# Gate, query and key projections of a decoder block in seven block products instead of eight, as a stage of their own

## The chip, the cores and the metric

One core of a Trainium2 chip runs the whole program. The metric is the device time of one execution in microseconds; shown are the median and the extremes of several executions, and one further execution that was profiled.

## The reference, cut to what matters

1024 tokens of width 1024 go through one layer: a gated linear attention (GLA) of 4 heads, three groups of dilated attention of 4 heads each, a mix of the two branches by sigmoid gates, and a mixture of 32 experts, 2 to a token. All is float32.

```python
h = rms_norm(x, norm1_g)
gq, gk, gv, gr, ga_lr = parts[:5]          # parts = split(h @ w_in): GLA q, k, v, output gate, decays
log_a = log_sigmoid(ga_lr @ w_gla_a2 + b_gla_a) / 16
o_gla = gla_chunked(heads(gq), heads(gk), heads(gv), heads(log_a))
y_gla = (rms_norm(o_gla) * silu(gr)) @ w_proj_gla
for window, dilation in ((128, 1), (512, 4), (2048, 16)):    # groups 0, 1, 2
    q, k, v = ...                          # q and k are normed per head
    o_g, m_g, d_g = dilated_group(q, k, v, ...)
y_att = combine(outs, maxes, dens) @ w_proj_attn
g_gla, g_att = split(sigmoid(h @ w_branch_gate + b_branch_gate))
x = x + (g_gla * y_gla + g_att * y_att) @ w_out
x = x + hier_moe(rms_norm(x, norm2_g), ...)
```

## The kernel before

Each float32 product is made of three matmuls on rounded parts: every operand is split into a high part and the rest, and `mm3` adds high by high, high by low and low by high into one PSUM tile of 128 partitions by 512 columns. A contraction over 1024 is eight k-steps, so 24 matmuls a tile. Weights come by way of `Weights`: SP issues the load of a unit of 128 by 1024 into `w_raw` (3 buffers); ScalarE rounds it (line 131) and VectorE takes the rest (line 132) into a `part` (5 buffers); `take(n)` hands out n units and prepares up to `ahead` more, four as a rule.

A planner lays the instructions of each engine out in one order, by their place in the program and by when it expects their inputs and buffers; it lets loads and stores run ahead of that place where a buffer is free. At run time every engine, and the queue of transfers that SP issues, keeps that order and waits at semaphores. `run`, `weave` and the generators set the place in the program: `weave(main, fill, n)` takes n steps of `fill`, a k-step of three matmuls each, for every step of `main`.

The stages, in order:

1. Eight token tiles are normed, transposed and split into the strips `hT`, while the first matmuls of the GLA values already run. The values (192 matmuls, strips stationary) stay in SBUF in `kb` tiles.
2. Decays of all four heads (`decays`), with head 0's queries and keys as filling. `heads(h)` makes the transposed queries and keys of a head with `columns`: the weights are stationary, the strips move; 96 matmuls a head.
3. `recur(h)`, the recurrence of head h in 16 steps, filled by `heads(h + 1)`, the last by `k_stage(2)`, the keys of dilated group 2.
4. `attention(g)` for g = 2, 1, 0: the values of the group (192 matmuls with nothing beside them), then queries, scores and values tile by tile, with the next group's keys, or at the end the first three tiles of `gr`, as filling. Outputs go to `oa_dram`, maxima and sums to `st_dram`.
5. `gr`: the GLA output gate, eight tiles, multiplied onto the GLA output into `ogs` (four `ka` and four `kb` tiles). From the maxima and sums of all groups come the factors `f_dram`.
6. The projection `yg` (line 694 on): 16 tiles of 12 matmuls, copied by ScalarE (line 702) and stored in `yg_dram`.
7. `together()` (line 707 on) combines the groups: for each of eight tiles three pairs of loads, of attention outputs and of factors that are spread over all partitions (lines 715 and 717), products on VectorE (line 719), two sums (722, 723) and a split into `oas`, in `ka` and `kb` tiles. It uses the nine `t2k` buffers of 512 columns. It stands in the program between `yg` and the gates.
8. Gates and mixing: for each c of 8, `gates(c, hf)` makes two tiles of 24 matmuls for either half of the tokens and a sigmoid; `mix` makes the attention projection (12 matmuls on four of the `oas`), the gated sum, and stores it in `zt_dram`. Gates of both halves stand ahead of the first `mix`.
9. `out_tile(n)` multiplies by `w_out`; beside it `route(n - 1)` norms the tile, computes router logits (line 884, copied at 887, turned at 890), picks experts and writes slots. For the last tile nothing stands beside it. The first loads of expert weights (`E.load`) are spread over these tiles.
10. 32 experts: a gather by GpSimd (line 992), transposes (line 999), three products with 72 matmuls in all, and an adding scatter.

Buffers are laid out as a stack: the tiles of stages 9 and 10 take the space of those of stages 1 to 8, and each waits only for the tiles that it overlaps.

## Time and profile before

| | |
|---|---|
| median of 3 runs | 1812.63 us (1810.82 to 1814.84) |
| profiled execution | 1810.6 us, of which the span of its instructions 1808.5 us |
| mean granted TensorE clock | 0.992 |
| TensorE, VectorE, ScalarE busy | 97%, 59%, 50% of the span |
| moved by transfers | 324.42 MB, mean 179 GB/s |

Times below count from the start of the span. A row of a timeline gives start, duration, engine, line and what is written from what; matmuls are pipelined, so their durations overlap and the distance of their starts is what one costs. An engine's idle time has a cost only where the engine that sets the end waits for it.

### The profile page before, as it was taken

What the parts mean: (1) busy time and instruction counts of PE and PEld (TensorE: products, weight loads), DVE (VectorE), ACT (ScalarE), POOL (GpSimd) and SP (SyncE); (2) the same over time, 40 slices, a digit from 0 to 9 for tenths busy, and PEclk for the clock granted to TensorE, in tenths of its full rate; (3) what the DMA queues carried; (4) which work ended last, traced back from release to release, by engine and by line L of the source; (5) the groups of instructions that cost most, each with busy time, mean ns of one, the idle gap of its engine ahead of it and who ended that gap; (6) DMA issues with size and microseconds to landing.
All of it is one profiled execution on the core that took longest, in us unless ns stands there. A gap on an engine that the chain in (4) does not pass through costs nothing.

```text
span 1808.5 us, 22835 instructions
## 1 busy us (share of the span) xinstructions
PE 1752.7 (97%) x8473; PEld 1477.2 (82%) x8473; DVE 1060.9 (59%) x1561; ACT 905.9 (50%) x1464; POOL 119.2 (7%) x110
## 2 busy tenths in 40 slices
PE   8999999999999999999999999979999999999995
PEld 6788899999998888887888877757777777777774
DVE  6475550342145225556222266679899989989884
ACT  6453441343244224532211142358888888787783
POOL 0000000000000000000000001121111111121110
PEclk9999999999999999999999999989999999999998
DMA  5111110121102111479222298489999999999991
GB/s 213 47 36 59 47 43 30 51 77 61 47 24 84 48 47 36 131 216 283 72 93 93 66 301 260 150 258 365 360 354 344 356 352 354 349 361 353 358 358 38
DMA packets 123216, 324.42 MB, mean 179 GB/s; under 512 B 25808, under 2 KB 42784, under 8 KB 123088
## 3 DMA queue, kind: packets, MB, share of 16 engines
q1 hardware_dynamic: 112512, 304.83, 47.8%
q0 software_dynamic: 10016, 17.78, 4.1%
q8 instruction: 67, 1.10, 0.2%
q14 instruction: 45, 0.37, 0.1%
q10 hardware_dynamic: 576, 0.34, 0.1%
HBM read 297.49 MB, written 42.43 MB: 188 GB/s over the span
## 4 chain that ended last, share of the span: by engine, by line
PE 85%; DVE 5%; DMA 4%; ACT 3%; issue 2%; SPq 0%; POOL 0%; POOLq 0%; DVEq 0%; ACTq 0%
PE acc L241 21%; PE acc L242 21%; PE acc L243 21%; PE mm L241 3%; PE mm L243 3%; PE mm L242 3%; PE mm L393 2%; PE mm L421 2%; DVE t2k L1011 2%; PE tp L999 1%; PE tp L339 1%; PE mm L594 1%; PE tp L1015 1%; DMA m_raw<-in_w_up_dram 1%; ACT part L131 1%
## 5 line engine op out<-in xcount | busy, mean ns | idle before, releaser
L132 DVE TENSOR_TENSOR part<-w_raw,part 128x1024 fp32r<-128x1024 f32 x114 | 139.3, 1222 | 258.9 <-ACT part L131 258.5
L241 PE MATMUL acc<-part,strip 128*128 128x512 f32 x640 | 276.6, 432 | 0.0
L242 PE MATMUL acc<-part,strip 128*128 128x512 f32 x640 | 257.4, 402 | 0.2 <-DVE part L132 0.2
L243 PE MATMUL acc<-part,strip 128*128 128x512 f32 x640 | 257.1, 402 | 0.0
L132 DVE TENSOR_TENSOR part<-m_raw,part 128x1024 fp32r<-128x1024 f32 x167 | 202.3, 1220 | 24.7 <-ACT part L131 23.6
L131 ACT CAST part<-m_raw 128x1024 fp32r<-128x1024 f32 x167 | 174.5, 1055 | 43.1 <-PE acc L243 31.0
L241 PE MATMUL acc<-strip,part 128*128 128x512 f32 x448 | 181.3, 405 | 1.2 <-ACT t2k L737 1.2
L242 PEld LDWEIGHTS acc<-part,strip 128*128 128x128 f32 x640 | 172.8, 270 | 10.3 <-DVE part L132 0.7
L243 PEld LDWEIGHTS acc<-part,strip 128*128 128x128 f32 x640 | 170.8, 267 | 11.4
L241 PEld LDWEIGHTS acc<-part,strip 128*128 128x128 f32 x640 | 170.7, 267 | 10.6 <-ACT part L131 0.5
L242 PE MATMUL acc<-strip,part 128*128 128x512 f32 x448 | 176.8, 395 | 0.0
L131 ACT CAST part<-w_raw 128x1024 fp32r<-128x1024 f32 x114 | 119.9, 1051 | 113.6 <-PE acc L243 94.5
L243 PE MATMUL acc<-strip,part 128*128 128x512 f32 x448 | 175.2, 391 | 0.0
L243 PE MATMUL acc<-part,xT 128*128 128x512 f32 x320 | 127.2, 398 | 0.0
L242 PE MATMUL acc<-part,xT 128*128 128x512 f32 x320 | 127.0, 397 | 0.0
L132 DVE TENSOR_TENSOR m_part<-m_raw,m_part 128x1024 fp32r<-128x1024 f32 x102 | 124.1, 1218 | 4.7 <-ACT m_part L131 4.4
L241 PE MATMUL acc<-part,xT 128*128 128x512 f32 x320 | 126.6, 395 | 0.0
L131 ACT CAST m_part<-m_raw 128x1024 fp32r<-128x1024 f32 x102 | 107.5, 1056 | 12.7 <-PE acc L243 8.3
L331 DVE TENSOR_REDUCE ss<-t2k 128x4 f32<-128x512 f32 x48 | 32.9, 685 | 133.4 <-ACT t2k L329 133.4
L241 PEld LDWEIGHTS acc<-strip,part 128*128 128x128 f32 x448 | 84.3, 188 | 20.6 <-ACT t2k L737 1.6
L243 PEld LDWEIGHTS acc<-strip,part 128*128 128x128 f32 x448 | 84.2, 188 | 18.3
L242 PEld LDWEIGHTS acc<-strip,part 128*128 128x128 f32 x448 | 84.4, 188 | 17.2 <-issue 1.2
(274 smaller groups left out, 3304.5 us busy)
## 6 DMA issues: line engine op xcount, KB each, us to landing
m_raw<-in_w_gate_dram SPq DMA_DIRECT2D x95, 512.0 KB
m_raw<-in_w_down_dram SPq DMA_DIRECT2D x89, 512.0 KB
m_raw<-in_w_up_dram SPq DMA_DIRECT2D x85, 512.0 KB
w_raw<-in_w_in_dram SPq DMA_DIRECT2D x52, 512.0 KB
w_raw<-in_w_mix_dram SPq DMA_DIRECT2D x32, 512.0 KB
n_raw<-in_w_up_dram SPq DMA_DIRECT2D x26, 512.0 KB
n_raw<-in_w_down_dram SPq DMA_DIRECT2D x22, 512.0 KB
w_raw<-in_w_gate_dram SPq DMA_DIRECT2D x17, 512.0 KB
```

The costliest lines, as they stand in the source:

```text
L131: self.copies.append(self.nc.scalar.copy(hi, raw))
L132: self.last = self.nc.vector.tensor_tensor(lo, raw, hi.bitcast(F32), op=OP.subtract)
L241: nc.tensor.matmul(ps, ah, bh, start=first, stop=False)
L242: nc.tensor.matmul(ps, ah, bl, start=False, stop=False)
L243: nc.tensor.matmul(ps, al, bh, start=False, stop=last)
L331: nc.vector.tensor_reduce(ss, sq.rearrange("p (h e) -> p h e", h=4), axis=AX.X, op=OP.add)
L339: nc.tensor.transpose(pt[:, 128 * h:128 * h + 128], sq[:, 128 * h:128 * h + 128], ident)
L393: nc.tensor.matmul(ps[:, h2, 128 * c:128 * c + 128], qT[:, 128 * h:128 * h + 128], kT[j][:, 128 * h:128 * h + 128], start=True, stop=True)
L421: nc.tensor.matmul(po[:, 128 * h:128 * h + 128], v[j][:, 128 * h:128 * h + 128], pTs[c][:, 128 * h:128 * h + 128], start=c == 0, stop=c == ...
L594: nc.tensor.matmul(pa[:n, t], ek[:, j], qt[:, t], start=True, stop=True)
L999: nc.tensor.transpose(pt[:, 128 * j:128 * j + 128], xg[:, 128 * k:128 * k + 128], ident)
L1011: prod = nc.vector.tensor_tensor(ap.rearrange("t (k p) -> t p k", k=4), a.rearrange("t (p k) -> t p k", k=4), pu.rearrange("t (p k) -> t p ...
```

## The change

The branch gates and the GLA queries and keys leave their stages and get one of their own, after the GLA values. It takes the weights in 12 pairs: two blocks of 128 output columns each (the two gates of one c, or two heads' queries or keys). With the pair as rows, the two halves of the contraction and the two halves of the tokens, each pair is a product of 2 by 2 blocks, done by Winograd's form of Strassen's method with seven block products in place of eight. `seven()` makes the seven left factors from the raw weights on VectorE and splits them; `sums(k)` makes, once for all pairs, four sums of strip parts and their splits, `T`; `winograd()` runs the products and puts the results together on VectorE from PSUM. Queries and keys go to `qk_dram`, sigmoids to `sig_dram`.

Around it: the GLA values go to `v_dram` and come back head by head; decays are made a head ahead within the recurrence; the recurrence is filled with the keys and the values of group 2, by the pattern 2, 2, 2, 1 and through DRAM for the values, which `attention(2)` then loads. The projection multiplies its tiles by the first gate, loaded into `s0`, on VectorE. Mixing runs over the halves of the tokens and then over c, with two loads and a store of 512 columns a round. The strips keep their space at the foot of the stack until the end of mixing. The router's product swaps its operands, which makes the copy and the transpose unnecessary. `warm(n)` issues n matmuls on a constant tile, at the start, beside the last tile's routing and before the experts.

```diff
             lst.append(units(sl(1024, 512), 4))
-            for h in range(4):
-                lst.append(units(np.concatenate([sl(128 * h, 128), sl(512 + 128 * h, 128)]), 2))
+            for h in (0, 2):
+                lst += [units(sl(512 * c + 128 * (h + j), 128), 1) for c in range(2) for j in range(2)]
+            for c in range(8):
+                lst += [wb[c:c + 1], wb[8 + c:9 + c]]
...
+    def raws(self, n):
+        if len(self.loaded) < n:
+            self.load(n - len(self.loaded))
+        got, self.loaded = [r for r, _ in self.loaded[:n]], self.loaded[n:]
+        return got
...
+def feed(main, fill, pattern):
+    i = 0
+    while True:
+        try:
+            next(main)
+        except StopIteration as e:
+            return e.value
+        for _ in range(pattern[i % len(pattern)]):
+            next(fill, None)
+        i += 1
...
     def room(i):
-        return raw.tile([128, 1024], F32, name="w_raw"), part if i < 81 else \
+        return raw.tile([128, 1024], F32, name="w_raw"), part if i not in (77, 78, 79) else \
             (lambda: p4.tile([128, 2, 1024], F32R, name="wo", bufs=3))
-    W = Weights(nc, [w_in[i] for i in range(52)] + [w_mix[i] for i in range(32)], room)
+    W = Weights(nc, [w_in[i] for i in range(68)] + [w_mix[i] for i in range(16)], room, 0)
...
+    still = consts.tile([128, 128], F32, name="still")
+    nc.vector.memset(still, 1.0)
+    def warm(n):
+        ps = acc()
+        for _ in range(n):
+            tc.keep_in_program_order(nc.tensor.matmul(ps[:, 0:128], still, still, start=True, stop=True))
...
+    warm(14)
...
+    units = W.take(4)
+    for b in range(NT):
+        ps = acc()
+        run(project(ps, 0, b, units))
+        t = t2k()
+        nc.scalar.copy(t, ps)
+        nc.sync.dma_start(v_dram[0, b // 2, :, 512 * (b % 2):512 * (b % 2) + 512], t)
...
+    tq = ts.enter_context(tc.tile_pool(name="tq", bufs=16))
+    Y = {(i, j): [tuple(p[:, 512 * j:512 * j + 512] for p in hT[4 * i + k]) for k in range(4)] for i in range(2) for j in range(2)}
...
+    def seven():
+        u, v = W.raws(2)
+        u1, u2, v1, v2 = u[:, :512], u[:, 512:], v[:, :512], v[:, 512:]
+        sums = [t2k() for _ in range(4)]
+        s1, s2, s3, s4 = sums
+        p = [part() for _ in range(4)]
+        W.copies.append(nc.scalar.copy(p[0][:, 0], u))
+        nc.vector.tensor_tensor(p[0][:, 1], u, p[0][:, 0].bitcast(F32), op=OP.subtract)
+        nc.vector.tensor_tensor(s1, v1, v2, op=OP.add)
+        nc.vector.tensor_tensor(s2, s1, u1, op=OP.subtract)
+        nc.vector.tensor_tensor(s3, u1, v1, op=OP.subtract)
+        nc.vector.tensor_tensor(s4, u2, s2, op=OP.subtract)
+        got = [(p[0][:, 0, :512], p[0][:, 1, :512]), (p[0][:, 0, 512:], p[0][:, 1, 512:])]
+        for n, (t, j) in enumerate(((s2, 1), (s3, 1), (s1, 2), (v2, 2), (s4, 3))):
+            c = slice(512 * (n % 2), 512 * (n % 2) + 512)
+            hi, lo = p[j][:, 0, c], p[j][:, 1, c]
+            split(hi, lo, t)
+            got.append((hi, lo))
+        W.load(2 - len(W.loaded))
+        return got
+    def winograd(blocks, scale, use):
+        a11, a12, s2, s3, s1, a22, s4 = blocks
+        def product(w, y):
+            ps = acc()
+            for k in range(4):
+                c = slice(128 * k, 128 * k + 128)
+                mm3(ps, (w[0][:, c], w[1][:, c]), y[k], k == 0, k == 3)
+            return ps
+        def plus(ps, t):
+            r = t2k()
+            nc.vector.scalar_tensor_tensor(r, ps, scale, t, op0=OP.mult, op1=OP.add)
+            return r
+        p1 = t2k()
+        nc.scalar.activation(p1, product(a11, Y[0, 0]), AF.Copy, scale=scale)
+        use(plus(product(a12, Y[1, 0]), p1), 0, 0)
+        x = plus(product(s2, T[2]), p1)
+        t = plus(product(s3, T[3]), x)
+        ps = product(s1, T[1])
+        use(plus(ps, t), 1, 1)
+        y = plus(ps, x)
+        use(plus(product(a22, T[4]), t), 1, 0)
+        use(plus(product(s4, Y[1, 1]), y), 0, 1)
+    T = {i: [] for i in (1, 2, 3, 4)}
+    def sums(k):
+        (h11, l11), (h12, l12), (h21, l21), (h22, l22) = (tuple(p.bitcast(F32) for p in Y[q][k]) for q in ((0, 0), (0, 1), (1, 0), (1, 1)))
+        def parts_of(i, v):
+            t = tq.tile([128, 2, 512], F32R, name="tq")
+            split(t[:, 0], t[:, 1], v)
+            T[i].append((t[:, 0], t[:, 1]))
+        def op(r, a, b, o):
+            nc.vector.tensor_tensor(r, a, b, op=o)
+        v, w = t2k(), t2k()
+        op(v, h22, h12, OP.subtract)
+        op(w, l22, l12, OP.subtract)
+        op(v, v, w, OP.add)
+        parts_of(3, v)
+        v2 = t2k()
+        op(v2, v, h11, OP.add)
+        op(v2, v2, l11, OP.add)
+        parts_of(2, v2)
+        v4 = t2k()
+        op(v4, h21, v2, OP.subtract)
+        op(v4, v4, l21, OP.add)
+        parts_of(4, v4)
+        v1, w1 = t2k(), t2k()
+        op(v1, h12, h11, OP.subtract)
+        op(w1, l12, l11, OP.subtract)
+        op(v1, v1, w1, OP.add)
+        parts_of(1, v1)
+    nxt = seven()
+    for k in range(4):
+        sums(k)
+    def keep_qk(c, h):
+        def use(t, j, hf):
+            nc.sync.dma_start(qk_dram[c, h + j, :, 512 * hf:512 * hf + 512], t)
+        return use
+    def keep_gate(c):
+        def use(t, j, hf):
+            nc.scalar.activation(t, t, AF.Sigmoid, bias=bgate[:, 8 * j + c:8 * j + c + 1])
+            nc.sync.dma_start(sig_dram[j, c, :, 512 * hf:512 * hf + 512], t)
+        return use
+    pairs = [(128.0 ** -0.5 if c == 0 else 1.0, keep_qk(c, h)) for h in (0, 2) for c in range(2)] + [(1.0, keep_gate(c)) for c in range(KT)]
+    for n, (scale, use) in enumerate(pairs):
+        blocks = nxt
+        if n < len(pairs) - 1:
+            nxt = seven()
+        else:
+            W.ahead = 4
+            W.fetch(4)
+        winograd(blocks, scale, use)
+    ts.close()
+    ph.close()
+    ph = ExitStack()
+    work = wide = ph.enter_context(tc.tile_pool(name="work", bufs=2, reuse_waits="tile"))
...
+    def v_stage(g, keep):
+        units = W.take(4)
+        for i in range(NT):
+            ps = acc()
+            yield from project(ps, g, i, units)
+            keep(i, ps)
...
+        if v is None:
+            v = []
+            def keep(i, ps):
+                if i == 0:
+                    run(last)
+                v.append(v[i - 1][:, 512:] if i % 2 else kb4())
+                nc.scalar.copy(v[i][:, :512], ps)
+            run(v_stage(g, keep))
...
         for c in range(2):
-            t = w4k()
-            for hf in range(2):
-                ps = acc()
-                yield from columns(ps, [(units[k // 4][0][:, 256 * (k % 4) + 128 * c:256 * (k % 4) + 128 * c + 128],
-                                         units[k // 4][1][:, 256 * (k % 4) + 128 * c:256 * (k % 4) + 128 * c + 128])
-                                        for k in range(KT)], hf)
-                nc.scalar.activation(t[:, 512 * hf:512 * hf + 512], ps, AF.Copy, scale=128.0 ** -0.5 if c == 0 else 1.0)
-            qk.append(t)
+            qk.append(w4k())
+            nc.sync.dma_start(qk[c], qk_dram[c, h])
...
+    def decays(h):
+        l, vh = kb4(), kb4()
+        for j in range(4):
+            nc.sync.dma_start(vh[:, 256 * j:256 * j + 256].rearrange("p (b e) -> p b e", b=2),
+                              v_dram[0, j].rearrange("p (b e) -> p b e", b=2)[:, :, 128 * h:128 * h + 128])
...
+    def keys_values(g, got):
+        got.append((yield from k_stage(g)))
...
+            t = t2k()
+            nc.scalar.copy(t, ps)
+            nc.sync.dma_start(v_dram[1, i // 2, :, 512 * (i % 2):512 * (i % 2) + 512], t)
...
+        yield from v_stage(g, keep)
...
+    got = []
+    fill = keys_values(2, got)
+    head = [feed(decays(0), fill, (8,))] + heads(0)
...
+        for i, _ in enumerate(main):
+            if i % 3 == 2 and other is not None:
+                try:
+                    next(other)
+                except StopIteration as e:
+                    out, other = out.append(e.value), None
+            yield
...
     for h in range(H):
-        _, qk = weave(recur(h, *qk), heads(h + 1) if h < H - 1 else k_stage(2), 2 if h < H - 1 else 4)
+        nxt = []
+        if h < H - 1:
+            following = heads(h + 1)
+        feed(both(recur(h, *head[0], *head[1:]), decays(h + 1) if h < H - 1 else None, nxt), fill, (2, 2, 2, 1))
+        if h < H - 1:
+            head = nxt + following
+    run(fill)
...
+    for j in range(NT // 2):
+        t = kb4()
+        nc.sync.dma_start(t, v_dram[1, j])
+        v2 += [t[:, :512], t[:, 512:]]
...
-        attention(g, *qk, after)
+        attention(g, *qk, v2 if g == 2 else None, after)
...
-        yt = w4k()
+        yt, s0 = w4k(), w4k()
+        nc.sync.dma_start(s0, sig_dram[0, c])
         for hf in range(2):
...
-            nc.scalar.copy(yt[:, 512 * hf:512 * hf + 512], ps)
+            cols = slice(512 * hf, 512 * hf + 512)
+            nc.vector.tensor_tensor(yt[:, cols], s0[:, cols], ps, op=OP.mult)
         nc.sync.dma_start(yg_dram[c], yt)
...
+    W.ahead = 1
+    wa = W.take(4)
+    for hf in range(2):
+        cols = slice(512 * hf, 512 * hf + 512)
+        for c in range(KT):
+            yt, sg, zt = t2k(), t2k(), t2k()
+            nc.sync.dma_start(yt, yg_dram[c, :, cols])
+            nc.sync.dma_start(sg, sig_dram[1, c, :, cols])
             ps = acc()
-            run(columns(ps, cut(u, 0, KT), hf))
...
-        nc.vector.tensor_tensor(sig[hf, 1], sig[hf, 1], ps, op=OP.mult)
-        nc.vector.tensor_tensor(zt[:, cols], sig[hf, 0], sig[hf, 1], op=OP.add)
-        nc.sync.dma_start(zt_dram[4 * hf:4 * hf + 4, :, c].rearrange("n p t -> p n t"), zt[:, cols].rearrange("p (n t) -> p n t", n=4))
...
+            for h, u in enumerate(cut(wa[c // 2], 4 * (c % 2), H)):
+                mm3(ps, u, oas[2 * h + hf], h == 0, h == H - 1)
+            nc.vector.tensor_tensor(sg, sg, ps, op=OP.mult)
+            nc.vector.tensor_tensor(zt, sg, yt, op=OP.add)
+            nc.sync.dma_start(zt_dram[4 * hf:4 * hf + 4, :, c].rearrange("n p t -> p n t"), zt.rearrange("p (n t) -> p n t", n=4))
...
     ph.close()
+    ph0.close()
...
-            nc.tensor.matmul(pl[:36, 0:128], wr_s[:, k], xts[k // 4][:, 128 * (k % 4):128 * (k % 4) + 128],
+            nc.tensor.matmul(pl[:, 0:36], xts[k // 4][:, 128 * (k % 4):128 * (k % 4) + 128], wr_s[:, k],
                              start=k == 0, stop=k == KT - 1)
-        lt = p4.tile([36, 128], F32, name="lt")
-        nc.vector.tensor_copy(lt, pl[:36, 0:128])
-        yield
-        pt = tp()
-        nc.tensor.transpose(pt[:, 0:36], lt, ident[:36, :36])
...
-        nc.vector.scalar_tensor_tensor(lg[:, 0:4], pt[:, 0:4], rs, br_s[:, 0:4], op0=OP.mult, op1=OP.add)
-        nc.vector.scalar_tensor_tensor(lg[:, 8:40], pt[:, 4:36], rs, br_s[:, 4:36], op0=OP.mult, op1=OP.add)
+        nc.vector.scalar_tensor_tensor(lg[:, 0:4], pl[:, 0:4], rs, br_s[:, 0:4], op0=OP.mult, op1=OP.add)
+        nc.vector.scalar_tensor_tensor(lg[:, 8:40], pl[:, 4:36], rs, br_s[:, 4:36], op0=OP.mult, op1=OP.add)
...
+    def waits():
+        yield
+        warm(15)
+        for _ in range(4):
+            yield
+        warm(4)
+        yield
...
-        _, xt = weave(route(n, xt), out_tile(n + 1) if n < NT - 1 else iter(()), 1)
+        _, xt = weave(route(n, xt), out_tile(n + 1) if n < NT - 1 else waits(), 1)
...
+    warm(36)
```

## Rows read from the trace of the kernel before

**Rows 1.** The page's shares: engine, busy us, share of the span, instructions.
```profile
PE 1752.7 (97%) x8473; PEld 1477.2 (82%) x8473; DVE 1060.9 (59%) x1561; ACT 905.9 (50%) x1464; POOL 119.2 (7%) x110
```
**Rows 2.** Stretches: length, then each engine's busy us, granted clock, transfer share, GB/s.
```profile
120.00:240.00 120.00, 120.00 (x697) 104.32 (x696) 67.46 (x147) 48.57 (x95) 0.00 (x0) 1.00 0.13 45
...
754.00:786.00 32.00, 32.00 (x141) 26.24 (x140) 20.61 (x35) 14.43 (x21) 0.00 (x0) 1.00 0.26 75
786.00:842.00 56.00, 55.56 (x243) 45.26 (x241) 35.56 (x44) 15.61 (x26) 0.00 (x0) 1.00 0.95 282
...
874.00:882.00 8.00, 8.00 (x37) 6.56 (x36) 3.04 (x4) 2.15 (x3) 0.00 (x0) 1.00 0.49 166
882.00:890.00 8.00, 8.00 (x37) 6.56 (x36) 2.77 (x4) 1.23 (x2) 0.00 (x0) 1.00 0.49 158
...
1176.00:1192.00 16.00, 4.56 (x18) 3.83 (x18) 8.03 (x28) 4.12 (x6) 3.54 (x4) 0.56 0.82 266
1200.00:1600.00 400.00, 396.72 (x1816) 316.02 (x1815) 364.83 (x370) 329.49 (x388) 60.02 (x42) 1.00 0.98 353
```
**Rows 3.** TensorE's timeline in the gate stage, the first and the last of 19 matmuls.
```profile
899.83 0.39 PE L241 MATMUL acc<-strip,part 128*128 128x512 f32 x1
...
903.95 0.39 PE L241 MATMUL acc<-ka,part 128*128 128x512 f32 x1
```
**Rows 4.** TensorE's timeline at the start; in brackets the idle time before.
```profile
7.81 1.97 PE L283 MATMUL tp<-mats,w4k 128*128 128x128 f32 x8 [7.81 <-DVE w4k L278]
...
11.82 0.63 PE L242 MATMUL acc<-part,strip 128*128 128x512 f32 x1
```
**Rows 5.** Places on the chain that ended last: start, us on it, what.
```profile
17.99 0.87 PE tp L283 x8
...
124.86 0.89 PE mm L606 x8
...
142.82 0.89 PE mm L606 x8
...
832.54 6.97 DMA t2k<-f_dram
...
1173.49 0.12 DVE lt L887
...
1173.66 0.26 PE tp L890
...
1182.27 7.11 DMA w4k<-h_dram,sidx
```
**Rows 6.** VectorE's timeline: after the norms, at three gating steps, at the seventh split.
```profile
40.91 0.42 DVE L247 TENSOR_TENSOR strip<-tp,strip 128x256 fp32r<-128x256 f32 x1 [0.44 <-ACT strip L246]
60.32 1.23 DVE L132 TENSOR_TENSOR part<-w_raw,part 128x1024 fp32r<-128x1024 f32 x1 [18.99 <-ACT part L131]
...
755.70 0.68 DVE L247 TENSOR_TENSOR ka<-t2k,ka 128x512 fp32r<-128x512 f32 x1
...
756.90 0.68 DVE L668 TENSOR_TENSOR t2k<-t2k,w4k 128x512 f32<-128x512 f32 x1
...
842.11 0.69 DVE L247 TENSOR_TENSOR ka<-t2k,ka 128x512 fp32r<-128x512 f32 x1
```
**Rows 7.** VectorE's instructions by form: count, busy us and mean ns, idle before them.
```profile
L132 DVE TENSOR_TENSOR part<-w_raw,part 128x1024 fp32r<-128x1024 f32 x114 | 139.3, 1222 | 258.9 <-ACT part L131 258.5 <-issue 0.3
...
L719 DVE TENSOR_TENSOR t2k<-t2k 128x512 f32<-128x512 f32 x24 | 22.8, 955 | 19.8 <-DMA t2k<-f_dram 19.8
...
L544 DVE TENSOR_TENSOR_SCAN ka<-t2k 128x128 f32<-128x128 f32 x32 | 11.0, 404 | 0.2
L745 DVE TENSOR_TENSOR t2k<-t2k,acc 128x512 f32<-128x512 f32 x16 | 11.0, 685 | 16.4 <-PE acc L243 16.4
```
**Rows 8.** TensorE's timeline where the gate matmuls begin.
```profile
824.92 0.39 PE L241 MATMUL acc<-strip,part 128*128 128x512 f32 x1
```

More of the change, by code (lines that the diff above doesn't have):

```diff
@@ L93, in _layout @@
     lst = [pair(wg, c) for c in range(0, 8, 2)]
-    for c in range(8):
-        lst += [wb[c], wb[8 + c]]
-        if c % 2 == 0:
-            lst.append(pair(wa, c))
+    lst += [pair(wa, c) for c in range(0, 8, 2)]
     out["w_mix"] = np.stack(lst + list(a["w_out"].reshape(8, 128, 1024)))
@@ L204, in w4k @@
     def w4k(shape=(128, 1024), dt=F32):
-        return work.tile(list(shape), dt, name="w4k", bufs=n4k)
+        return wide.tile(list(shape), dt, name="w4k", bufs=n4k)
     def ka4(shape=(128, 1024), dt=F32):
@@ L357, in k_stage, with attention @@
         return kT, last
-    def attention(g, kT, last, after):
+    def v_stage(g, keep):
[4 more added lines that the diff above has]
+            keep(i, ps)
+    def attention(g, kT, last, v, after):
         bias = w4k((128, 4, 256))
@@ L363, in attention @@
         sd = work.tile([128, NT, 2, 4], F32, name="sd", bufs=2)
-        units = W.take(4)
-        v = []
-        for i in range(NT):
-            ps = acc()
-            run(project(ps, g, i, units))
-            if i == 0:
-                run(last)
-            if i % 2 == 0:
-                t = kb4()
-            v.append(t[:, 512 * (i % 2):512 * (i % 2) + 512])
-            nc.scalar.copy(v[i], ps)
+        if v is None:
[6 more added lines that the diff above has]
+            run(v_stage(g, keep))
         units = W.take(4)
@@ L478, in attention @@
             nc.sync.dma_start(st_dram[g], sn)
-    units = W.take(4)
-    v = []
-    for b in range(NT):
-        ps = acc()
-        run(project(ps, 0, b, units))
-        if b % 2 == 0:
-            t = kb4()
-        v.append(t[:, 512 * (b % 2):512 * (b % 2) + 512])
-        nc.scalar.copy(v[b], ps)
     wr = t2k((128, 128))
```

102 lines of the change are left out of this document (40 added, 62 removed).

## The prediction

> **What bounds the kernel now.** I read the shares first: TensorE is busy 97% of the span [rows 1]. Then the stretches [rows 2], for idle time and for what fills the other engines. Through the recurrence (120 to 240 us) TensorE never waits, with VectorE at 56%; from 786 to 842 us it loses 0.44 us although the transfer engines are full; through the experts, with transfers full again, under 1%. Only between the last tile and the experts (1176 to 1192 us) is it idle, busy 4.56 of 16 us at a granted 0.56. So a matmul that goes is worth its own time, unless something that it covered comes out. What it covers I looked for on the chain of waits and in VectorE's order of time.
>
> **The removed matmuls.** A pair of weight blocks took 8 products of 4 k-steps of 3 matmuls, 96; now 7, 84. Of 12 pairs (8 of gates, 4 of queries and keys), 144 matmuls of 512 columns go. In the gate stage 18 of them start within 903.95 - 899.83 = 4.12 us [rows 3], 0.229 us each: -33.0 us. The rows hold the stationary and moving kinds of the new phase, so I keep that rate. All other matmuls of 512 columns only move.
>
> **The opening.** Early matmuls last 0.63 us where the gate stage has 0.39 [rows 3, 4], and eight transposes take 1.97 us [rows 4], later 0.87 [rows 5]: the start runs at 1.2 GHz. Fourteen dummy matmuls are put ahead of it. Some seven slow matmuls at 0.2 us: -1.5 us; from 0, if the first tile's transfers hold it anyway, to -2.5.
>
> **Sums of the block phase.** VectorE's last instruction on the normed strips starts at 40.91 us, and it then rests 19 us [rows 6]: that is the cover. Every sum reads the last token tile, so none starts before 41.3 us. Each k takes 10 adds or subtractions and 4 splits, 14 instructions at 0.60 us start to start (755.70 to 756.90 are two steps [rows 6]), 8.4 us; four k take 34 us, and the five half splits of the first weights, whose buffers come free only as the value stage ends, 3 us: until about 78 us. The value stage's matmuls end near 62 us, two products need no sums (24 x 0.229 = 5.5 us), and the third wants its fourth k at 69 us, which VectorE has at about 74. Then the product results, which VectorE must read out of three PSUM buffers, queue behind the sums still left. I take +8 us: from 0 (results first, sums in between) to 14 (sums and the next pair's weights all ahead). Later pairs are covered: 1.22 + 9 x 0.60 + 7 x 0.69 = 11.5 us of VectorE [rows 6, 7] against 84 x 0.229 = 19.2 us of TensorE. The phase's weights and stores, 25 MB in 231 us, are 110 GB/s where 282 have been carried [rows 2]: nothing.
>
> **The recurrence.** Its filling goes from 2 steps of 3 matmuls for each of its own to 1.75, and decays, key norms and weight splits come beside it. A half of a head takes 142.82 - 124.86 = 18.0 us [rows 5], a head 36; at 56% VectorE has 20 us of that, 18 without splits. Decays add two instructions of 0.69 and eight scans of 0.40 us [rows 7], 4.6; norms about 5, splits 2.4: 30 us, 83%. TensorE has no wait there at 56%; I allow +3 us, from 0 to 10. Keys, queries and values are loaded a head ahead, on SP's queue, where only the stores of keys and values stand before them: nothing, or a few us at the first head, inside that bound. The value stage that leaves group 2's attention costs the same in its new place.
>
> **Where the gates ended.** This is the largest unknown. The stage that combines the three attention groups fetches 24 pairs of transfers and made the seventh of its eight tiles at 842.11 + 0.69 us [rows 6]; the projection stage ended at 824.9, where gate matmuls began [rows 8]. The 96 gate matmuls ahead of the first mixing product were the cover. They are gone, and mixing wants four of the combined tiles at once, the seventh among them. Unchanged transfers leave 842.8 - 824.9 - 2 (the first nine matmuls) = 16 us of wait. More come in: half of the sigmoids beside the projection, then two loads and a store of 256 KB for each of 16 rounds of 12 x 0.229 = 2.75 us. From 786 us on I count 22 pairs, 11.5 MB, at 282/0.95 = 297 GB/s, and 21.5 MB of others (4.2 of products stored, 2.6 of sigmoids not yet fetched, 4.2 + 4.2 + 4.2 for mixing, 2.1 of weights) at the 330 GB/s of a full share that 874 to 890 us show [rows 2]: 39 + 65 = 104 us, to 890. Matmuls alone would end at 824.9 + 192 x 0.229 = 868.9. So +21 us; from 2 (transfers drawn ahead into 754 to 786 us, whose share is 0.26 [rows 2]) to 45 (the second rival). VectorE now reads the projection's results too, in order behind instructions that waited 19.8 us for transfers [rows 7]; three PSUM buffers cover 5.5 us of a wait, and the rest is caused by the same transfers, already counted.
>
> Nine buffers serve the rounds. A load took 6.97 us from its issue [rows 5]; with VectorE's steps of 0.69 us a round holds them for about 7.7 + 8.4 + 7.7 us, 2.6 us over nine, just under 2.75. The Trainium skill ("DMA: Bandwidth & Descriptors", Anatomy of one DMA) puts a transfer at some 2 us plus its bytes over 436 GB/s, an estimate of 2.6 us for 256 KB, by which a round needs 1.2 us and the buffers never bind. The loaded queue here shows 6.97, so I keep the row.
>
> **The end of routing.** A copy and a transpose leave the chain of each tile (from 1173.49 until 1173.66 + 0.26 [rows 5]): 0.4 us at the last tile, covered by output matmuls at the others. Dummy matmuls keep TensorE at work there. The 4.56 us in 1176 to 1192 would be 2.6 us at the full level (0.56 of 4.56), eight further transposes some 1.1 us less (1.97 against 0.87 [rows 4, 5]): with the 0.4, and a little for the matmuls after them, -4 us, from -2 (the dummies end too early) to -6. The 36 before the experts last about 8 us, if a product of this width costs 2 x 0.11 us as two transposes do [rows 5]; that is inside the wait for the first gather, 7.11 us from 1182.27 [rows 5], within 1 us. Experts and the loads that wait for their buffers start that much earlier, so it is passed on in full.
>
> **The sum**: -33.0 - 1.5 + 8 + 3 + 21 - 4 = -6.5 us. The profiled execution took 1810.6 us (span 1808.5), 2.0 below the median of 1812.6; from the one 1804, from the other 1806. I predict **1805 us**.
>
> **Rivals.**
> *Mixing opens without a wait* (2 in place of 21). The combining stage was in no hurry, with 96 gate matmuls behind it; buffers or the queue's order, not bandwidth, held it before 786 us. For it: the share of 0.26 just before. Against it: 0.95 right after. 19 us less: 1786.
> *Transfers bound projection and mixing outright*; this is the one on the other side. Its place is 786 to 890 us. The strips lie free there now, so expert and output tiles that are laid over them can be fetched at once: up to 13 transfers of 0.5 MB, 6.8 MB, 21 us at 330 GB/s, ahead of what mixing waits for. Then 21 becomes 42 to 45 and the time 1829. The slower sign starts from 32 us of wait on. For it: a full share already stands there; against it: loads for later stages may be ordered behind.
> *Sums and recurrence at their upper ends* (14 and 10 for 8 and 3): 13 us more, 1818.
> *The block form saves nothing*: if half of the weights of each pair are late by 2.8 us, 12 pairs eat the 33 us and the time is 1838. The 7.7 us of VectorE that each pair leaves over speak against it; I count it with the third.
>
> **Chances.** Forecast 0.44 (1796 to 1812 by its own terms), open mixing 0.24 (1778 to 1796), transfers 0.24 (1814 to 1834), late sums 0.08. 0.2% of 1812.6 is 3.6 us, about what can be told from no change. Faster: 0.24 and three quarters of 0.44, 0.57. Same: a fifth of 0.44, a tenth of 0.24, half of 0.08, 0.15. Slower: the rest, 0.28. The range leaves a tenth out on each side: 1782 to 1830.
>
> **What would show it.** 144 fewer matmuls at 0.229 us; in the block phase's first pair TensorE waiting for sums about 5 us at the third product, and for results to be read after it, and no wait in later pairs; no idle stretch of more than a few us in the recurrence; 16 us or more without TensorE between the last projection matmul and the first whole mixing product, with the transfer share near 1; no granted 0.5 between router and experts. I am wrong if TensorE runs through into mixing, if the share falls while it waits there (then buffers or order hold it), or if the new phase waits in each pair.

## The result, and the profile after

The changed kernel took 1963.2 us (1959.7 to 1966.9, 4 runs) beside 1813.7 us of the kernel before (1810.8 to 1817.9, 4 runs): a ratio of 1.083, 95% interval 1.081 to 1.085. It is 150 us slower; forecast were 1805 us, and the range ended at 1830. Line numbers below are those of the changed kernel; an edited kernel's differ by a few lines.

The page's shares after [rows 1]: engine, busy us, share, instructions.
```profile
PE 1790.4 (91%) x8459; PEld 1490.7 (76%) x8459; DVE 1197.9 (61%) x1790; ACT 1085.2 (55%) x1632; POOL 117.1 (6%) x110
```
TensorE lies idle for 174 us of the span of 1964.7, where before it was 56. ScalarE is busy for 179 us more, which no step of the prediction accounts for. Four stretches [rows 2] show where:
```profile
120.00:240.00 120.00, 120.00 (x516) 96.67 (x515) 70.14 (x104) 36.83 (x55) 0.00 (x0) 1.00 0.31 107
...
360.00:560.00 200.00, 171.57 (x912) 154.60 (x912) 111.10 (x247) 136.18 (x200) 0.00 (x0) 0.94 0.19 65
...
1112.00:1190.00 78.00, 51.10 (x159) 36.52 (x160) 24.87 (x35) 3.70 (x5) 0.00 (x0) 0.80 0.54 166
1190.00:1212.00 22.00, 2.40 (x9) 1.70 (x8) 8.44 (x13) 2.92 (x5) 2.94 (x5) 0.59 0.65 203
```
The block phase (first row) runs without a pause, as forecast. The recurrence (second) loses 28 of 200 us, and there ScalarE, not VectorE, is the fuller engine: 68%. Mixing (third) loses 27 of 78 us with a transfer share of 0.54, so the transfers are not full; and behind it (last row) TensorE stands still for 20 us.

What fills ScalarE, in its groups of instructions (count, busy us, mean ns, idle before) and in its order of time inside the recurrence:
```profile
L283 ACT ACT_TABLE_LOAD x53 | 68.0, 1283 | 0.9
L284 ACT ACT_TABLE_LOAD x47 | 60.3, 1283 | 0.8
...
372.76 1.28 ACT L283 ACT_TABLE_LOAD   x1
374.06 0.30 ACT L283 ACTIVATE rs<-ss,eps 128x4 f32<-128x4 f32 x1
374.37 1.28 ACT L284 ACT_TABLE_LOAD   x1
375.67 0.20 ACT L284 ACTIVATE rs<-rs 128x4 f32<-128x4 f32 x1
```
Lines 283 and 284 are the logarithm and the exponential of `rsqrt`. Work of 0.30 and 0.20 us carries 1.28 us of load each. In all there are 130 loads, 167 us, where the kernel before has 6.

The waits of TensorE name the other places (who waited for what, us in all, times, longest); first the recurrence, then the opening of mixing, its rounds, and the wait behind it:
```profile
PE mm L742 <- DVE t2k L738: 19.1, 9, 3.5
...
PE acc L265 <- ACT ka L279: 20.6, 3, 11.5
PE acc L265 <- DVE t2k L931: 5.2, 1, 5.2
...
PE acc L265 <- DVE t2k L931: 20.7, 12, 2.6
...
PE acc L265 <- ACT z L279: 19.6, 1, 19.6
```
The first row names VectorE, but its product takes one of ScalarE's exponentials, which stand behind the loads; the first experiment tests this reading. In the opening the transfer share is near 1:
```profile
1080.00:1120.00 40.00, 16.63 (x52) 11.31 (x50) 29.38 (x38) 4.79 (x8) 0.00 (x0) 0.73 0.95 279
```
Ahead of the last wait, the loads of the first output tile stand on SP's queue right behind the last round's store, though the tokens of that tile were stored by the eighth round of sixteen:
```profile
1206.69 0.37 SPq L933 DMA_DIRECT2D zt_dram<-t2k  x1
1207.10 1.49 SPq L968 DMA_DIRECT2D zr<-zt_dram  x3
```

At the start of the block phase, VectorE's last work ahead of its rest and the first behind it [rows 6], and the four longest waits of TensorE that follow, from its timeline:
```profile
45.59 0.68 DVE L386 TENSOR_TENSOR t2k<-w_raw,t2k 128x512 f32<-128x512 f32 x1
67.46 0.69 DVE L280 TENSOR_TENSOR part<-t2k,part 128x512 fp32r<-128x512 f32 x1 [21.19 <-ACT part L279]
...
76.63 0.80 PE L265 MATMUL acc<-tq,part 128*128 128x512 f32 x1 [4.74 <-ACT tq L279]
...
85.31 0.79 PE L265 MATMUL acc<-tq,part 128*128 128x512 f32 x1 [6.18 <-ACT tq L279]
...
93.98 0.80 PE L265 MATMUL acc<-tq,part 128*128 128x512 f32 x1 [6.18 <-ACT tq L279]
...
102.66 0.80 PE L265 MATMUL acc<-tq,part 128*128 128x512 f32 x1 [6.17 <-ACT tq L279]
```
VectorE's rest of 19 us before, which was to be the cover of the sums, is still there, now 21 us long. The stretch from 66 us until all sums are made, TensorE's waits in it, and two of the matmuls of a later pair [rows 3], thirteen steps apart:
```profile
66.00:120.00 54.00, 24.65 (x72) 16.09 (x71) 46.85 (x75) 16.84 (x28) 0.00 (x0) 0.62 0.15 52
...
PE acc L265 <- ACT tq L279: 23.3, 4, 6.2
PE acc L265 <- ACT t2k L413: 4.1, 1, 4.1
PE acc L266 <- DVE tq L280: 1.9, 4, 0.5
...
199.83 0.39 PE L266 MATMUL acc<-strip,part 128*128 128x512 f32 x1
...
202.86 0.40 PE L267 MATMUL acc<-strip,part 128*128 128x512 f32 x1
```
In mixing, the queue that SP issues, and one load on the chain that ended last [rows 5]:
```profile
1135.64 0.37 SPq L933 DMA_DIRECT2D zt_dram<-t2k  x1
1136.05 1.23 SPq L927 DMA_DIRECT2D t2k<-sig_dram  x1
1137.33 0.43 SPq L926 DMA_DIRECT2D t2k<-yg_dram  x1
1141.18 0.37 SPq L933 DMA_DIRECT2D zt_dram<-t2k  x1
...
1136.05 3.59 DMA t2k<-sig_dram
```
A round's store waits for its result, and the next round's load of the gate is issued only behind it: every 5.5 us one round, where twelve matmuls are 2.75. The chain passes through such a load in nearly every round.

### The profile page after: what moved, and what is told of

Read it like the earlier page. It is cut to its first block, busy times and chain, and to the rows that moved or that the text cites. A ratio compares the mean times of both kernels' runs of the same rounds, so it can differ in the third digit from the quotient of the medians.

```text
span 1964.7 us, 23578 instructions
## 1 busy us (share of the span) xinstructions
PE 1790.4 (91%) x8459; PEld 1490.7 (76%) x8459; DVE 1197.9 (61%) x1790; ACT 1085.2 (55%) x1632; POOL 117.1 (6%) x110
## 4 chain that ended last, share of the span: by engine, by line
PE 63%; ACT 11%; DVE 11%; DMA 10%; issue 4%; SPq 0%; POOL 0%; DVEq 0%; POOLq 0%; ACTq 0%
PE acc L265 16%; PE acc L266 16%; PE acc L267 16%; PE mm L265 2%; DMA t2k<-sig_dram 2%; PE mm L266 2%; PE mm L267 2%; DMA m_raw<-in_w_gate_dram 2%; ACT L283 2%; DVE part L131 2%; ACT part L130 1%; DVE t2k L435 1%; ACT w4k L568 1%; DMA n_raw<-in_w_down_dram 1%; DVE m_part L131 1%
## 5 line engine op out<-in xcount | busy, mean ns | idle before, releaser
L265 PE MATMUL acc<-part,strip 128*128 128x512 f32 x640 | 282.0, 441 | 1.0 <-ACT part L130 1.0
L266 PE MATMUL acc<-part,strip 128*128 128x512 f32 x640 | 264.7, 414 | 1.2 <-DVE part L131 1.2
L267 PE MATMUL acc<-part,strip 128*128 128x512 f32 x640 | 262.2, 410 | 0.0
L131 DVE TENSOR_TENSOR part<-w_raw,part 128x1024 fp32r<-128x1024 f32 x90 | 109.6, 1221 | 99.7 <-ACT part L130 99.2
L130 ACT CAST part<-w_raw 128x1024 fp32r<-128x1024 f32 x90 | 93.9, 1049 | 53.4 <-PE acc L267 46.2
L409 DVE SCALAR_TENSOR_TENSOR t2k<-acc,t2k 128x512 f32<-128x512 f32 x84 | 56.9, 690 | 96.7 <-PE acc L267 88.1
L496 DVE TENSOR_TENSOR t2k<-acc,rs 128x512 f32<-128x512 f32 x48 | 33.2, 692 | 118.9 <-ACT rs L284 118.9
L265 PE MATMUL acc<-tq,part 128*128 128x512 f32 x192 | 78.9, 411 | 27.4 <-ACT tq L279 23.3
L265 PE MATMUL acc<-strip,part 128*128 128x512 f32 x208 | 83.2, 400 | 0.0
L266 PE MATMUL acc<-strip,part 128*128 128x512 f32 x208 | 82.4, 396 | 0.0
L267 PE MATMUL acc<-strip,part 128*128 128x512 f32 x208 | 82.3, 396 | 0.0
```

Source lines behind the costliest of these rows:

```text
L130: self.copies.append(self.nc.scalar.copy(hi, raw))
L131: self.last = self.nc.vector.tensor_tensor(lo, raw, hi.bitcast(F32), op=OP.subtract)
L265: nc.tensor.matmul(ps, ah, bh, start=first, stop=False)
L266: nc.tensor.matmul(ps, ah, bl, start=False, stop=False)
L267: nc.tensor.matmul(ps, al, bh, start=False, stop=last)
L409: nc.vector.scalar_tensor_tensor(r, ps, scale, t, op0=OP.mult, op1=OP.add)
```

## The experiments

"Before" is the kernel before, run on the same chip. A time is a median; the ratio to before has its 95% interval.

**Tables.** One preload, behind the last gate of the block phase:
```diff
-            nc.scalar.activation(t, t, AF.Sigmoid, bias=...)
+            gates.append(nc.scalar.activation(t, t, AF.Sigmoid, bias=...))
...
         winograd(blocks, scale, use)
+    pre = nc.scalar.preload_act_table_set("natural_log_exp_and_others")
+    tc.add_manual_dep(pre.ins, gates[-1].ins.name, ...)
```


> One activation-table preload (the set with Ln and Exp) is put on ScalarE behind the last sigmoid of the block phase; nothing else changes. Theory A (the sigmoid evicted the set, and each Ln and Exp of the recurrence and of the attention stages then loaded its own): the 130 loads of 1.28 us become 8, TensorE's busy share from 360 to 560 us goes from about 85% to over 95%, and the time falls by 60 to 70 us, to 1893 to 1903 us. Rival B (the filling of 1.75 steps and the added decays, norms and splits on VectorE hold the recurrence; the loads lie beside it): the loads go all the same, ScalarE's busy time falls by 156 us, and the time falls by less than 20 us.

1903.5 us, ratio 1.050 (1.048 to 1.052): 59.7 us less, theory A. The stretch of the recurrence in this kernel:
```profile
360.00:560.00 200.00, 199.69 (x1124) 188.61 (x1123) 123.55 (x272) 97.06 (x213) 0.00 (x0) 1.00 0.22 76
```
TensorE waits 0.3 us in 200, though VectorE has more to do in the same time: the filling of 1.75 steps, with decays and norms beside it, makes it wait for nothing here. Then the other way round, in the kernel before:
```diff
         nc.scalar.copy(v[b], ps)
+    spoil = small.tile([128, 1], F32, name="spoil")
+    nc.scalar.activation(spoil, v[NT - 1][:, 0:1], AF.Sigmoid)
```


> The kernel before, with one sigmoid of one column on ScalarE behind the value stage, whose result nobody uses; nothing else changes. Theory A (one sigmoid without the table set put back is the cause by itself, whatever the new fillings are): about 130 table loads in place of 6, and 45 to 65 us more, 1858 to 1878 us. Rival B (the loads cost so much only because the changed recurrence has more on VectorE and ScalarE, and in the kernel before they lie in free time): under 20 us more.

1871.0 us, ratio 1.031 (1.028 to 1.034), 58 us more for one sigmoid of a single column. The stretch that ran without a pause before [rows 2]:
```profile
120.00:240.00 120.00, 111.56 (x619) 91.65 (x618) 59.41 (x135) 54.52 (x86) 0.00 (x0) 0.90 0.09 31
```
So the loads are the cause by themselves. The Trainium skill ("ScalarE: Activation LUTs", What ACT_TABLE_LOAD costs) gives 1283 ns for a load, and the trace agrees; it adds 1380 ns of drain to each switch, which the rows do not show (372.76 to 374.06 is 1.30 us from the load to the next instruction, and the second load starts at 374.37, as that instruction ends). The same page (Table sets: the hidden batching unit) counts one load for a logarithm followed by an exponential, since one set holds both. The trace of the changed kernel disagrees: loads stand before both, 53 and 47 times. With the set preloaded by name behind the last sigmoid, those hundred are gone.

**The sums, first try.**
```diff
-    nxt = seven()
-    for k in range(4):
+    for k in range(3):
         sums(k)
+    nxt = seven()
+    sums(3)
```


> In the program's order the sums of token tiles 0 to 2 stand ahead of the first pair's weight splits, tile 3's behind them. Theory A (the splits, which wait for part buffers of the value stage, stood ahead of the sums on VectorE and ScalarE and kept 21 us of VectorE's rest from being used): VectorE works on sums from 44 us on, TensorE's waits between 66 and 100 us fall from 27 us to under 8, and the time falls by 20 to 33 us, to 1930 to 1943 us. Rival B (the three buffers of results that VectorE must read, behind whatever sums are left, hold the first pair in either order): under 10 us.

1964.1 us: no change, and a miss. VectorE rested as long as before. ScalarE's order of time shows why:
```profile
64.62 0.59 ACT L365 COPY t2k<-acc 128x512 f32<-128x512 f32 x1 [4.91 <-PE acc L267]
65.11 0.62 ACT L279 CAST tq<-t2k 128x512 fp32r<-128x512 f32 x1
```
The first half of a sum's split stands behind the eight copies of the value stage, the last of which waits for TensorE until 64.6 us; VectorE's second half waits for that. The theory named the wrong queue.

**The sums, among the value stage's products.**
```diff
         nc.sync.dma_start(v_dram[0, b // 2, ...], t)
+        if b == 3:
+            sums(0)
+        elif b == 4:
+            sums(1)
+        elif b == 6:
+            sums(2)
```


> In the program's order the sums of token tiles 0 to 2 stand among the value stage's products (behind products 3, 4 and 6), tile 3's behind the first pair's weight splits; nothing else changes. The run before this one showed VectorE at rest until 65 us although the sums stood ahead of the weight splits. Theory A (ScalarE takes its instructions in order too, and the first half of a sum's split stood behind the eight copies of the value stage, the last of which waits for TensorE until 64.6 us): VectorE works on sums from 42 us on, TensorE's waits between 66 and 112 us fall from 29 us to under 10, the time falls by 20 to 35 us, to 1928 to 1944 us. Rival B (VectorE's 34 us of sums and 12 us of weight splits and results are too much in any order): under 10 us.

1952.6 us, ratio 1.077 (1.075 to 1.079), 11 us less. VectorE now works on sums from 43 us on, as theory A has it, and the waits of the first pair fell from 29.3 to 11.7 us; but the time fell by less than the theory's 20 us. Part of the gain is lost again in the wait ahead of the decays' products, which rose from 6.4 to 12.1 us:
```profile
PE acc L670 <- DVE t2k L280: 12.1, 1, 12.1
```
Its weight is loaded into a buffer that a gate's store must leave first, so the load can't run ahead of the phase's end. In the 205 us from the decays on, 876 matmuls now start at a granted 0.86, where 932 did at 0.94; what lowers the clock there, no run isolates.

**Mixing.** Loads two rounds ahead:
```diff
+    for r in range(2):
+        fetched(r)
+    for r, (hf, c) in enumerate(rounds):
+        fetched(r + 2)
+        yt, sg = got[r]
...
-            nc.vector.tensor_tensor(zt, sg, yt, op=OP.add)
+        nc.vector.tensor_tensor(yt, sg, yt, op=OP.add)
```


> In mixing the two loads of a round are issued two rounds ahead of its products, and the result overwrites the loaded projection tile in place of a third tile; same bytes, same arithmetic. Theory A (SP's queue takes its instructions in order, the store of a round stands ahead of the next round's loads, so every round shows the whole way of a load): a round goes from 5.5 us to 2.8 to 3.3, and the time falls by 30 to 42 us, to 1921 to 1933 us. Rival B (the transfers are short of bandwidth or spoilt by the store's small pieces): rounds stay above 4.5 us and the time falls by less than 15 us.

1925.6 us, ratio 1.062 (1.060 to 1.064), 37.6 us less, theory A. Two stores of neighbouring rounds are now 2.80 us apart:
```profile
1135.95 0.37 SPq L944 DMA_DIRECT2D zt_dram<-t2k  x1
...
1138.75 0.37 SPq L944 DMA_DIRECT2D zt_dram<-t2k  x1
```
The wait behind mixing fell too, from 19.6 to 11.0 us, and the opening's waits stayed (24.3 us). The edit also takes two buffers a round in place of three. No run parts that from the earlier loads, but the queue's own rows speak for the order: before the edit it stood 51.4 us in 14 waits for the results that its stores carry, with the next loads behind them.

**The three edits at once.**

> The three edits together. If they are three separate causes the gains add up: 110 to 145 us, 1818 to 1853 us, close to the kernel before or a little above it. If one of them hid another (a wait that moves on), the sum is missed by 20 us or more.

1862.8 us, ratio 1.028 (1.025 to 1.030): 100.4 us less, where the three alone gave 59.7 - 0.9 + 37.6 = 96.4. Tables and mixing are separate causes; the range expected was missed because the sums' edit gave nothing.

**Fewer bytes at the opening of mixing.** The gated products stay in the strips:
```diff
-        yt, s0 = w4k(), w4k()
+        if c % 2 == 0:
+            ygs.append(strip.tile([128, 2, S], F32R, name="strip"))
+        yt, s0 = ygs[c // 2][:, c % 2].bitcast(F32), w4k()
...
-        nc.sync.dma_start(yg_dram[c], yt)
```


> The kernel with the three edits, and besides the projection's gated products stay in the strips' memory, which is free by then: 8 stores of 512 KB and 16 loads of 256 KB go. Theory A (transfers bound the opening of mixing: share 0.93 to 0.94 from 980 to 1060 us): TensorE's wait of 24 us there falls by 10 to 18 us, and the time from 1862.8 to 1845 to 1853 us. Rival B (the order of SP's queue and of VectorE holds the opening, not the bytes): under 5 us.

1846.1 us, ratio 1.019 (1.017 to 1.021), 16.8 us less than with the three edits, theory A. In the opening TensorE's waits go from 24.2 us to 9.5:
```profile
PE acc L264 <- ACT ka L278: 6.1, 1, 6.1
PE acc L264 <- DVE t2k L948: 2.2, 1, 2.2
PE acc L264 <- DVE strip L898: 1.2, 2, 0.7
```
The run doesn't part bytes from order: the eight stores that went had held SP's queue for 21.1 us, until their results were there, with the combining stage's loads behind them.

**All edits**: tables, early sums, strips with four rounds ahead, and
```diff
-    nc.scalar.dma_start(wr, w_alr)
+    nc.gpsimd.dma_start(wr, w_alr)
...
+        if n == 0:                       # the first output tile, in z_tile
+            zh, zl = w4k((128, KT, 128), F32R), w4k((128, KT, 128), F32R)
+            ...
+                nc.scalar.dma_start(zr, zt_dram[n, :, c])
```


> All edits: tables, sums among the value stage's products, mixing's loads four rounds ahead with the products in the strips, the first output tile's loads on ScalarE's queue into other buffers, the two small loads ahead of the recurrence on GpSimd's queue. If the causes are separate: 1862.8 less 25 to 33 (sums), 10 to 18 (strips), 4 (small loads), 5 to 9 (first output tile), 1799 to 1819 us; the kernel before is at 1812.8. What is still above 1812.8 would be transfers at the opening of mixing.

1822.4 us, ratio 1.006 (1.004 to 1.008): 3 us above what was expected. The wait of 19.6 us behind mixing is gone: the longest there are 2.5 and 1.7 us. The decays' products waited 12.4 us for their weight again, so GpSimd's queue did not help. The buffer was late, not the queue; the load on GpSimd is released by a gate's store:
```profile
321.45 0.76 POOL L659 DMA_DIRECT2D t2k<-in_w_alr_dram  x1 [320.18 <-DMA sig_dram<-t2k]
```

**The two small parts of the change, alone in the kernel before.** Fourteen dummies ahead of the opening (`warm(14)`):

> The kernel before with the fourteen dummy products ahead of its opening, nothing else. By the prediction -1.5 us (0 to -2.5). Rival: the dummies end before the first tile has come, the clock falls again, or they delay the first transposes: -0.5 to +3 us.

1814.2 us, ratio 0.999 (0.998 to 1.001): neither the forecast nor its rival can be told from no change. The first eight transposes take 1.09 us in place of 1.97 [rows 4] but begin at 8.09 us, not 7.81. The routing alone:
```diff
-            nc.tensor.matmul(pl[:36, 0:128], wr_s[:, k], xts[k // 4][...], ...)
+            nc.tensor.matmul(pl[:, 0:36], xts[k // 4][...], wr_s[:, k], ...)
...
+    warm(36)
```


> The kernel before with the changed routing alone: logits with the tokens as rows (no copy, no transpose), one step more between, and dummy products in the last tile's route (15 and 4) and ahead of the experts (36). By the prediction -4 us (-2 to -6). Rival (the first gather, 7.1 us from its issue, ends it as before, and dummies hold up what comes behind them): -1 to +2 us.

1806.2 us, ratio 0.996 (0.995 to 0.998): 7 us less by the medians, 4.0 by the spans of the profiled executions (1804.5 for 1808.5). From 1176 to 1192 us the granted clock is now 0.95 in place of 0.56 [rows 2]. Whether the swapped operands or the dummies give the gain, no run separates.

**A weight that is early, and GpSimd for three of the ten additions.**
```diff
+    wa = consts.tile([128, KT, 2, 16], F32R, name="wa")     # loaded and split in the opening
...
-        op(v1, h12, h11, OP.subtract)
-        op(w1, l12, l11, OP.subtract)
-        op(v1, v1, w1, OP.add)
+        op(v1, h12, h11, OP.subtract, nc.gpsimd)
+        op(w1, l12, l11, OP.subtract, nc.gpsimd)
+        op(v1, v1, w1, OP.add, nc.gpsimd)
```


> The kernel with all edits (1822.4 us, 0.57% above the kernel before) and two more: the small weight of the decays is loaded and split in the opening into memory of its own (its load stood behind a gate's store whose buffer it reuses: 12.4 us of TensorE's wait at the end of the block phase), and three of the ten additions of each k of the sums are made by GpSimd, which does nothing else there. Theory: 11 us from the first, 4 to 9 us from the second (third product's wait of 6.1 us and that of 4.1 us behind it), 1802 to 1809 us, 0.2 to 0.6% below the kernel before. Rival: GpSimd and VectorE hinder each other on the same memory, VectorE's steps of 0.60 us become longer, and the second gives nothing or a loss: 1811 to 1816 us.

1815.7 us, ratio 1.001 (1.000 to 1.003). The wait for the weight is gone (no wait from 120 us to 370), but the first pair waits 13.6 us where it was 11.7. VectorE beside GpSimd and, later, alone; then GpSimd:
```profile
48.87 3.49 DVE L380 TENSOR_TENSOR t2k<-strip 128x512 f32<-128x512 f32 x2
...
78.44 1.28 DVE L380 TENSOR_TENSOR t2k<-strip 128x512 f32<-128x512 f32 x2
...
48.42 1.68 POOL L380 TENSOR_TENSOR t2k<-strip 128x512 f32<-128x512 f32 x1 [1.23 <-DVE tq L279]
50.18 1.62 POOL L380 TENSOR_TENSOR t2k<-t2k 128x512 f32<-128x512 f32 x1
```
Two of VectorE's additions, the rows at 48.87 and 78.44, take 3.49 us beside GpSimd's and 1.28 alone. The Trainium skill ("GPSIMD Engine Reference", Key points) says that the two engines share their way into SBUF and contend where VectorE reads two SBUF inputs; the trace agrees. The same kernel without GpSimd's additions:

> The kernel with all edits and the early small weight, all additions on VectorE. If GpSimd's additions hindered VectorE (two of its additions took 2.45 and 3.49 us beside one of GpSimd, for 1.28 alone), this kernel is 1 to 4 us faster than the one with them, 1809 to 1814 us; if they did not, it is 2 to 5 us slower, 1818 to 1821 us.

1809.8 us, ratio 0.999 (0.998 to 1.000): 0.27% less, some 5 us; so GpSimd's help cost more than it took over.

**Plain products in the same place** (against the run with GpSimd's additions):
```diff
-        winograd(blocks, scale, use)
+        for j, unit in enumerate(W.take(2)):
+            for hf in range(2):
+                ps = acc()
+                run(columns(ps, cut(unit, 0, KT), hf))
```


> The same kernel with plain products in the block phase in place of the seven: 1152 matmuls for 1008, no sums, no half splits, everything else (place of the phase, its stores, all later stages) as it is. If the block form gives what its matmuls cost: 12 x 96 x 0.229 = 264 us against 235 us and some 8 us of waits left at its start, so this kernel is 18 to 29 us slower than the one with seven products. Rival (sums, results and stores of the seven products cost as much as the twelve matmuls of a pair): within 8 us of it.

1828.9 us, ratio 1.009 (1.006 to 1.011), 13.1 us above the seven products with their 13.6 us of waits: below what was expected, by about those waits and the low clock beside them (granted 0.81 from 66 to 120 us, here 1.00).

**The order in the first pair.**
```diff
+    rest = sums(3)
-    nxt = seven()
-    sums(3)
+    nxt = seven(lambda: next(rest))      # behind its first split: the sums for products 3 and 4
...
         use(plus(product(a12, Y[1, 0]), p1), 0, 0)
+        if mid:
+            mid()                        # the rest of the last tile's sums
         x = plus(product(s2, T[2]), p1)
         t = plus(product(s3, T[3]), x)
+        if late:
+            late()                       # the second pair's splits
```


> All edits without GpSimd's additions, and the first pair in another order: behind the first split of its weights come the sums of the last tile that its third and fourth products want, then the other splits, the first two results, the rest of those sums, two more results, and only then the second pair's splits. Theory (order): the third product's wait goes from 6.1 us to under 2 and that for the second buffer of results from 4.1 us to under 1; 6 to 11 us less than the run without it, 1800 to 1806 us, 0.4 to 0.7% below the kernel before. Rival (amount of work): the same 10 us of waits, spread over other products, 1808 to 1813 us.

1804.4 us, ratio 0.995 (0.994 to 0.996): faster than both kernels, by 0.5% for the one before. That kernel with the new routing alone had 0.996 (0.995 to 0.998), and the two are not told apart: once mended, the phase itself shows no gain clear of the noise. The first pair's waits, 11.7 us without this order, are 7.1:
```profile
PE acc L264 <- DVE t2k L454: 4.4, 2, 3.8
PE acc L264 <- ACT t2k L458: 1.7, 1, 1.7
PE acc L266 <- DVE part L279: 1.0, 1, 1.0
```
The time is 5.4 us less than without it, just under the theory's 6 to 11. The third product waits 1 us, as the theory has it; the longest wait, 3.8 us, is now the second pair's first product, for a result that VectorE has yet to read, which is the rival's part.

## Why the prediction was wrong

*What bounds the kernel now* was right about the kernel before. Its own condition, that a matmul is worth its time unless something that it covered comes out, is what then happened.

*The removed matmuls*: right in kind, a little large. 144 are gone. In the new phase the thirteen steps from 199.83 to 202.86 us are 0.233 each, where I kept 0.229 [rows 3]; 1152 at 0.229 less 1008 at 0.233 is 28.7 us, for 33.0. Plain products in the same place take 0.233 too, so the rate belongs to the place; why is open.

*The opening*: -1.5 forecast, between -4 and +2 by the interval.

*Sums of the block phase*: +8 forecast, with 14 as the bound; measured were 29.3 us of waits, at a granted 0.62. The work was sized rightly: the waits for the sums come 8.7 us apart, for the 8.4 us a k forecast. The start was wrong. The step took VectorE's rest for cover and looked at VectorE's queue alone. ScalarE makes the first half of each split, and its copies of the value stage stand ahead. An idle stretch is cover only if every engine that the work passes through can take it then. The bound "sums and the next pair's weights all ahead" assumed that the sums start at 41 us; no split of a sum came before 65 us, neither in the changed kernel nor in the first try.

*The recurrence*: +3 forecast, 0.3 us of waits once the tables are put back, so the step's own terms held; VectorE is busy for 62% there, less than the 83% that it had. What failed is what the step left out: the sigmoids moved ahead of the recurrence, and with them the change of the table set. In the kernel before, the gates stood behind all logarithms and exponentials but those of the router's stage, and a preload stood behind them. A move past an engine's state was costed at nothing; it was the largest part, 60 of the 150 us.

*Where the gates ended*: +21 forecast, 25.8 us of waits in the opening. Place and size were right, and the transfer share was full, as the step has it. Without the projection's stores and reloads, 8.4 MB, the waits are 14.7 us shorter; how much of that is bytes, and how much the stores' place in the queue, stays open, and so does how far the agreement in size is luck.

*Nine buffers serve the rounds*: wrong; it was costed at nothing. The step compared how long buffers are held with how often they are needed, and never asked when the load is issued. On SP's queue it stood behind the round before's store, so that its whole way of 3.6 us showed in nearly every round; the share of 0.54 is the sign that I had named for this case. With what the wait behind mixing lost, it was 37.6 us. The estimate of 2.6 us a transfer beside that step goes by a fit that the Trainium skill ("DMA: Bandwidth & Descriptors", Anatomy of one DMA) gives for transfers issued by GpSimd; these were issued by SP, and the one shown took 3.59 us.

*Behind mixing* was missing from the steps: 19.6 us until the first output tile, 11.0 when the rounds are quick. In the kernel before, gates and a delayed mixing product stood there; now the tile's loads wait on SP's queue for the last round's store.

*The end of routing*: -4 forecast, with -6 as the bound; -7 measured (-10 to -4.5 by the interval).

Of the rivals, none gives 1963. "Transfers bound projection and mixing outright" had the sign and the stage, but with a share that is full; it was full in the opening alone, and half in the rounds.

Added up: -28.7 and -7 from what was to gain; 60 from the tables, 29 from the sums, 6 from the decays' weight, 26 from the opening of mixing, 21 in its rounds and 20 behind them: +126. Some 24 us are left. Part of them stands beside the low granted clock. From 66 to 120 us 72 matmuls keep TensorE busy for 24.65 us, where 0.233 us each make 16.8; and quick rounds gave 37.6 us, where the waits that went are 20.7 and 8.6. Each is some 8 us, by estimate; the rest is not separated.

What the form is worth, with most of its waits gone, is the last version against plain products, ratios 0.995 and 1.009: 1.4%, 25 us. Routing gives 0.4%. All else that came with the phase (its own place, its results in DRAM, the new order around it) costs 1.009 against 0.996, 23 us; no run takes that apart. The two nearly cancel.

## What to carry to other kernels

When a stage moves, list what it leaves behind in each engine, not only how busy it keeps it: one sigmoid ahead of logarithms and exponentials cost 58 us by the table loads that followed. Idle time of one engine is cover only if the other engines of the same operand, and the queues that load and store it, can also reach that work then; look at the order in each. And price a round of load, compute and store by the place of the next load in the queue before pricing it by buffers or bandwidth.

## What was not expected of the hardware

A table load takes 1.28 us, and logarithms and exponentials in turn brought a hundred of them here, although a set with both exists and serves both when it is preloaded. GpSimd's additions of 1.6 us stretch two of VectorE's from 1.28 to 3.49 us. Matmuls of the same shape and operand kinds took 0.229 us in the gate stage before [rows 3] and 0.233 in the block phase, seven products or plain ones, both at a granted 1.00.
